# Score products of three attention layers: 64 contracted rows widened to 128

## The chip, the cores and the metric

One core of one Trainium2 chip runs the whole program. The metric is the device time in microseconds of one execution, the median of several runs.

## What is computed

The program is two small transformer blocks over one sequence of 512 tokens with 1024 features, all in float32. The first block has a dilated attention layer and a state-space (S5) layer; the second has a differential attention layer, an HGRN layer, a sliding-window layer and another differential layer, each followed by a feed-forward part. The change touches the scores of the attention layers alone, which the reference computes with 64 features a head:

```python
logits = jnp.einsum('bnqrhe,bnkrhe->bnrhqk', qs, kw, ...) * scale + bias      # dilated, 3 groups
s = jnp.einsum('bmqd,bmkd->bmqk', q[:, :, qs:ke], k[:, :, :ke])               # differential
s = jnp.einsum('bnqhgd,bnkhd->bnhgqk', q, kb)                                 # sliding window
```

After the scores come a bias, a softmax over the keys and the product with the values.

## The kernel before

Activations stand transposed in SBUF, features on the 128 partitions and 512 tokens in the free dimension. Matrix products of weights are made from two parts of each operand, a rounded high part and the remainder (the type F32R), in three products (`mm3`, L167 to L169). A projection (`projF_steps`) makes one block of 128 features by 512 tokens out of 8 times 3 such products and hands the PSUM tile to an epilogue on ScalarE or VectorE.

The 16 heads are taken in four quarters of four heads. A block of 128 features holds two heads, e = 0 on partitions 0 to 63 and e = 1 on 64 to 127. For every quarter there is a chain of projections (q, k, v) and an `attend` generator with eight steps, one for each of four query blocks and two pairs of heads; a step makes the scores of step i, transposes the probabilities of step i - 1 and multiplies those of step i - 2 with the values. `weave` interleaves the projections of what comes next (the fill) with the attend steps of what is there, in the order in which TensorE is to run them; a scheduler keeps to that order where dependencies and free tiles allow. Softmax goes through VectorE (bias and minimum, L474 or L805) and ScalarE (exponential, L477 or L807).

- **Dilated layer** (`dilated`, plain float32 scores). `project_q` (L554 to 557) writes one tile Q of 128 partitions by 2 blocks by 512 tokens, one ScalarE operation for each block. `products` multiplies rows 64e to 64e + 63 of Q and K: for group 0 one product of 128 or 256 keys for each head (L589), for the other two groups two products of 128 keys for each head (L593). There are 12 q projections (4 quarters, 3 groups), 24 blocks in all.
- **Differential layers** (`diff_attention`, two of them). `pack_q` (L868 to 876) writes for each head a tile half with the high part of q on the head's own 64 rows and the low part on the other 64. `pack_k` (L878 to 886) writes the high part of k on both halves (the copy is L886) and the low part on the head's own half alone; one tile `kl` holds the low parts of both blocks of a quarter. `packed_scores` then makes two products: 128 rows of q against the high part of k (L891), and the head's own 64 rows against the low part (L892), accumulated in PSUM.
- **Sliding layer** (`swa`). The same two products through `pair_scores`; its low part of k already stands on both halves. Its value products write 64 columns of the array at a time (L978); they do not change.

The tiles of q, k, v, bias, low parts, outputs and products (`self.g`) share one pool `gp` of 16 slots; a tile waits for a free slot, and a slot comes free with the last use of what it held. Projections share three PSUM buffers (`ps_mm`), scores two (`ps_sc`). Bias tiles come by DMAs on SP's queue (L461).

Of the kernel before, what the change touches and what calls it, by code (L numbers as in the profile page):

```python
# [11 lines left out]
F32 = mybir.dt.float32  # L12
F32R = mybir.dt.float32r
ACTF = mybir.ActivationFunctionType
ALU = mybir.AluOpType
AX = mybir.AxisListType

P = 128
S = 512
# [31 lines left out]
class Core:  # L51
# [454 lines left out]
    def dilated(self, w_in, d1, g_out, rest):  # L506


        nc = self.nc
        def col(which, g, q):  # L510
            c0 = which * 3072 + g * 1024 + q * 256
            return w_in[:, c0:c0 + 256]

        def view(ps, g):
            return ps if g == 0 else ps.rearrange("p (j r) -> p r j", r=4)

        def dst(t, m, g):
            return t[:, m, :] if g == 0 else t[:, m, :].rearrange("p (r j) -> p r j", r=4)
# [33 lines left out]
                yield  # L552

        def project_q(qd, g, t):  # L554
            t["q", g] = Q = self.g([P, 2, S], name="q")
            yield from self.projF_steps([col(0, g, qd)], 256,
                                        lambda m, ps: nc.scalar.mul(dst(Q, m, g), view(ps, g), -0.125))

        def project_k(qd, g, t):
            t["k", g] = K = self.g([P, 2, S], name="k")  # L560
# [12 lines left out]
        def attend(qd, g, t):  # L573
            st = t["st", g] = self.small([P, TB, 2, 4], f"st{g}", 2)
            O = t["O", g] = self.g([P, TB, 256], name="O")
            b = t["b0"] if g == 0 else self.g([P, 4, 256], name="b12")
            if g:
                self.bias_tile(b[:, :, 0:128], d1, 4 * qd, 4, 384 + 127, 128)
                self.bias_tile(b[:, :, 128:256], d1, 4 * qd, 4, 640 + 127, 128)

            def scores(i):
                u, m = divmod(i, 2)
                us, hs = slice(u * P, u * P + P), slice(2 * m, 2 * m + 2)

                def products(e, ps):
                    r = slice(64 * e, 64 * e + 64)
                    if g == 0:
                        k0 = max(0, u - 1) * P
                        nc.tensor.matmul(ps[:, :u * P + P - k0], lhsT=t["q", 0][r, m, us],  # L589
                                         rhs=t["k", 0][r, m, k0:u * P + P], start=True, stop=True)  # L590
                        return
                    for i in range(2):
                        nc.tensor.matmul(ps[:, i * P:i * P + P], lhsT=t["q", 1 + i][r, m, us],  # L593
                                         rhs=t["k", 1 + i][r, m, us], start=True, stop=True)

                return self.pair_scores(products, b[:, hs, :], lo(i), st[:, u, 0, hs], st[:, u, 1, hs], None)

            def lo(i):
                return P if g == 0 and i < 2 else 0

            def V(i, e, k):
                u, m = divmod(i, 2)
                c = slice((2 * m + e) * 64, (2 * m + e) * 64 + 64)
                return t["v", 0][:, u - 1 + k, c] if g == 0 else t["v", 1 + k][:, u, c]

            def values(i, pt):
                u, m = divmod(i, 2)
                po = self.psum([P, P], self.ps_av, "av")
                for e in range(2):
                    for k in range(lo(i) // P, 2):  # L610
                        nc.tensor.matmul(po[:, 64 * e:64 * e + 64], lhsT=pt[:, e, k, :], rhs=V(i, e, k),
                                         start=(k == lo(i) // P), stop=(k == 1))
                (nc.vector.tensor_copy if m else nc.scalar.copy)(O[:, u, m * P:m * P + P], po)

            for i, _ in enumerate(self.attend_pairs(8, scores, lo, values)):
                if (i + 1) * 8 // 10 > i * 8 // 10:
                    self.tick()
                yield
# [145 lines left out]
    def diff_attention(self, w_in, lam, subln, d2, lam_init, g_out, rest):  # L764

        nc = self.nc
# [15 lines left out]
        def project(qd, out):  # L782
            cs = lambda i, n: w_in[:, i * 1024 + qd * 256 + n.start:i * 1024 + qd * 256 + n.stop]
            V = self.g([P, TB, 256], name="v")
            yield from self.projT_steps(cs(2, slice(0, 256)),
                                        lambda tp, ps: nc.scalar.copy(V[:, 2 * tp:2 * tp + 2, :], ps))
            kl = self.g([P, 2, S], F32R, "kl")
            for m in range(2):
                bt = self.g([P, 2, S], name="bt")
                self.bias_tile(bt, d2, 4 * qd + 2 * m, 2, 127, S)  # L790
                q, kh = self.g([P, 2, S], F32R, "q"), self.g([P, 2, S], F32R, "kh")
                epi = lambda i, ps: (self.pack_k(ps, kh, kl[:, m, :]) if i else self.pack_q(ps, q))
                ms = slice(m * P, m * P + P)
                yield from self.projF_steps([cs(0, ms), cs(1, ms)], 256, epi)
                out.append((bt, q, kh, kl[:, m, :], V))

        def scores(bt, Q, Kh, Kl, V, u, m):
            nk = u * P + P
            nm, l = self.small([P, 2], "nm"), self.small([P, 2], "l")
            ss = []  # L800
            for e in range(2):
                ps = self.psum([P, S], self.ps_sc, "sc")
                s = self.t2([P, S], name="s")
                self.packed_scores(ps[:, :max(nk, 256)], Q, Kh[:, e, :], Kl, e, slice(u * P, nk), slice(0, max(nk, 256)))
                nc.vector.tensor_tensor_reduce(out=s[:, :nk], in0=ps[:, :nk], in1=bt[:, e, S - nk:], scale=1.0,  # L805
                                               scalar=3e38, op0=ALU.add, op1=ALU.min, accum_out=nm[:, e:e + 1])
                nc.scalar.activation(out=s[:, :nk], in_=s[:, :nk], func=ACTF.Exp, scale=-1.0,  # L807
                                     bias=nm[:, e:e + 1], accum_out=l[:, e:e + 1])
                ss.append(s)
            r1, f2 = self.small([P, 2], "r1"), self.small([P, 1], "f2")  # L810
            nc.vector.reciprocal(out=r1, in_=l)
            nc.vector.tensor_tensor(out=f2, in0=l[:, 0:1], in1=r1[:, 1:2], op=ALU.mult)
            nc.vector.tensor_tensor(out=f2, in0=f2, in1=nlam, op=ALU.mult)
            a = ss[0]
            nc.vector.scalar_tensor_tensor(out=a[:, :nk], in0=ss[1][:, :nk], scalar=f2, in1=a[:, :nk],
                                           op0=ALU.mult, op1=ALU.add)
            return a, r1
# [60 lines left out]
    def pack_k(self, ps, kh, kl):  # L878


        nc = self.nc
        for e in range(2):
            r, o = (slice(64 * i, 64 * i + 64) for i in (e, 1 - e))
            nc.scalar.copy(kh[r, e, :], ps[r, :])
            nc.vector.tensor_tensor(out=kl[r, :], in0=ps[r, :], in1=kh[r, e, :].bitcast(F32), op=ALU.subtract)  # L885
            nc.vector.tensor_copy(kh[o, e, :], kh[r, e, :])  # L886

    def packed_scores(self, ps, q, kh, kl, e, qs, ks):

        r = slice(64 * e, 64 * e + 64)  # L890
        self.nc.tensor.matmul(ps, lhsT=q[:, e, qs], rhs=kh[:, ks], start=True, stop=False)  # L891
        self.nc.tensor.matmul(ps, lhsT=q[r, e, qs], rhs=kl[r, ks], start=False, stop=True)  # L892

    def heads_by_quarters(self, project, attend, rest, n, period, tail, after):

# [15 lines left out]
    def swa(self, w_in, sinks, d2, g_out, rest):  # L911
        nc = self.nc
# [29 lines left out]
        def attend(qd, bq):  # L942
# [4 lines left out]
            def scores(i):  # L947
                u, m = divmod(i, 2)
                k0 = max(0, u - 1) * P
                hs = slice(2 * m, 2 * m + 2)  # L950
                sink = ns[:, 4 * qd + 2 * m:4 * qd + 2 * m + 2]
                nm, l, es = (self.small([P, 2], n) for n in ("nm", "l", "es"))

                def products(e, ps):
                    self.packed_scores(ps, Q[m], Kh[:, kv, :], Kl[:, kv, :], e, slice(u * P, u * P + P),
                                       slice(k0, k0 + 256))

                s = self.pair_scores(products, b0[:, hs, :], lo(i), nm, l, sink)
                nc.vector.tensor_tensor(out=es, in0=nm, in1=sink, op=ALU.subtract)
                nc.scalar.activation(out=es, in_=es, func=ACTF.Exp)  # L960
                nc.vector.tensor_tensor(out=es, in0=es, in1=l, op=ALU.add)
                nc.vector.reciprocal(out=es, in_=es)
                for e in range(2):
                    nc.vector.tensor_scalar(out=s[:, e, lo(i):], in0=s[:, e, lo(i):], scalar1=es[:, e:e + 1],
                                            scalar2=None, op0=ALU.mult)
                return s
# [647 lines left out]
```

## Time and profile before

| | us |
|---|---|
| median of 3 runs (lowest, highest) | 3721.05 (3717.48, 3723.71) |
| profiled execution | 3716.22 |
| its span, first to last instruction | 3714.3 |
| TensorE busy with products | 3647.3 (98%) |
| VectorE busy | 2206.8 (59%) |
| ScalarE busy | 1389.1 (37%) |
| GpSimd busy | 131.7 (4%) |

The profiler models the end of a product, so that products overlap in its records and a busy share near 100% does not say how fast they follow each other. The distance from one start to the next is what a product costs; the timeline gives these starts. A form such as "64\*128 64x256" is 64 contracted rows by 128 stationary columns, with 256 moving columns. Stages of the program by time: dilated layer about 20 to 720 us, first differential layer 1040 to 1300, sliding layer 2455 to 2620, second differential layer 3030 to 3290.

### The profile page before, as it was taken

The page shows a single profiled execution, that of the slowest core. Times are in us where ns is not written, and L with a number is a line of the kernel's source. Part 1 is how long each engine was busy: PE and PEld are TensorE (multiplying, and loading weights), DVE is VectorE, ACT ScalarE, POOL GpSimd, SP SyncE. Part 2 cuts the span into 40 slices and gives each one's busy share as a digit, 9 for nine tenths or more (in the row PEclk, how much of TensorE's full clock was granted, in tenths as well). Part 3 has the DMA queues.
Part 4 walks back from the last instruction along what each step waited for, and adds up shares of the span by engine and source line. Part 5 has one row for each costly group of instructions (what it writes and reads, how often), then busy time and mean ns, then how long its engine had stood idle before and what let it go on. Part 6 is the DMA issues. An engine that isn't in the chain of part 4 may idle for free. (4 is left out here: it accounts for less than half of the span.)

```text
span 3714.3 us, 49214 instructions
## 1 busy us (share of the span) xinstructions
PE 3647.3 (98%) x19511; PEld 3038.2 (82%) x19511; DVE 2206.8 (59%) x4701; ACT 1389.1 (37%) x2409; POOL 131.7 (4%) x191
## 2 busy tenths in 40 slices
PE   8999999889999999999999999999999999999999
PEld 7878787777777788889988888886888898788888
DVE  5677684555656744465778444657644556774445
ACT  4333333435344333234553222344322244432222
POOL 0000000010000100000000000000000000010000
PEclk9999999989999999999999999999999999999999
DMA  6234332465533222322212323321232243222322
GB/s 174 79 114 116 103 109 90 163 199 149 109 103 87 74 91 91 113 96 81 69 61 84 101 96 102 108 80 52 81 112 91 97 115 91 69 91 91 102 97 69
DMA packets 331806, 371.46 MB, mean 100 GB/s; under 512 B 37958, under 2 KB 268390, under 8 KB 331576
## 3 DMA queue, kind: packets, MB, share of 16 engines
q1 hardware_dynamic: 328064, 356.93, 31.6%
q0 software_dynamic: 3328, 11.14, 1.0%
q8 instruction: 153, 2.51, 0.3%
q14 instruction: 77, 0.63, 0.1%
q10 hardware_dynamic: 184, 0.26, 0.0%
HBM read 339.18 MB, written 29.10 MB: 99 GB/s over the span
## 5 line engine op out<-in xcount | busy, mean ns | idle before, releaser
L167 PE MATMUL mm<-xh,wh 128*128 128x512 f32 (+1 forms) x2488 | 943.8, 380 | 4.0 <-ACT wh L136 2.5
L168 PE MATMUL mm<-xl,wh 128*128 128x512 f32 (+1 forms) x2488 | 932.1, 375 | 3.0 <-DVE xl L137 3.0
L169 PE MATMUL mm<-xh,wl 128*128 128x512 f32 (+1 forms) x2488 | 931.2, 375 | 0.6 <-DVE wl L137 0.6
L137 DVE TENSOR_TENSOR wl<-wr,wh 128x2048 fp32r<-128x2048 f32 x270 | 633.7, 2348 | 467.9 <-ACT wh L136 457.2
L136 ACT CAST wh<-wr 128x2048 fp32r<-128x2048 f32 x270 | 536.9, 1989 | 812.9 <-PE mm L169 427.6
L167 PEld LDWEIGHTS mm<-xh,wh 128*128 128x128 f32 x2488 | 472.4, 190 | 86.4 <-issue 4.0
L169 PEld LDWEIGHTS mm<-xh,wl 128*128 128x128 f32 x2488 | 472.3, 190 | 83.6 <-DVE wl L137 1.6
L168 PEld LDWEIGHTS mm<-xl,wh 128*128 128x128 f32 x2488 | 472.9, 190 | 82.3 <-DVE xl L137 3.5
L168 PE MATMUL mm<-wl,uh 128*128 128x512 f32 x1024 | 399.2, 390 | 0.0
L167 PE MATMUL mm<-wh,uh 128*128 128x512 f32 x1024 | 398.8, 389 | 0.0
L169 PE MATMUL mm<-wh,ul 128*128 128x512 f32 x1024 | 398.4, 389 | 0.0
L167 PE MATMUL mm<-wh,xh 128*128 128x256 f32 (+1 forms) x1088 | 321.2, 295 | 0.0
L168 PE MATMUL mm<-wl,xh 128*128 128x256 f32 (+1 forms) x1088 | 317.5, 292 | 0.0
L169 PE MATMUL mm<-wh,xl 128*128 128x256 f32 (+1 forms) x1088 | 316.9, 291 | 0.0
L320 DVE TENSOR_TENSOR h<-h,mm 128x512 f32<-128x512 f32 x256 | 174.3, 682 | 233.0 <-PE mm L169 232.9
L167 PEld LDWEIGHTS mm<-wh,uh 128*128 128x128 f32 x1024 | 192.2, 188 | 39.9
L169 PEld LDWEIGHTS mm<-wh,ul 128*128 128x128 f32 x1024 | 192.3, 188 | 39.7
L168 PEld LDWEIGHTS mm<-wl,uh 128*128 128x128 f32 x1024 | 192.3, 188 | 39.4
L167 PEld LDWEIGHTS mm<-wh,xh 128*128 128x128 f32 x1088 | 209.7, 193 | 5.3 <-ACT xh L136 1.1
L168 PEld LDWEIGHTS mm<-wl,xh 128*128 128x128 f32 x1088 | 209.5, 193 | 4.0 <-issue 1.2
L169 PEld LDWEIGHTS mm<-wh,xl 128*128 128x128 f32 x1088 | 209.3, 192 | 3.1 <-issue 0.4
L136 ACT CAST uh<-t 128x512 fp32r<-128x512 f32 x128 | 79.4, 621 | 189.3 <-DVE t L350 189.3
(375 smaller groups left out, 4762.8 us busy)
## 6 DMA issues: line engine op xcount, KB each, us to landing
wr<-in_w_up_dram SPq DMA_DIRECT2D x64, 1024.0 KB, 5.5
wr<-in_w_down_dram SPq DMA_DIRECT2D x64, 1024.0 KB, 5.1
wr<-in_attn_w_in_dram SPq DMA_DIRECT2D x40, 1024.0 KB, 5.1
wr<-in_da_w_in_dram SPq DMA_DIRECT2D x32, 512.0 KB, 5.3
wr<-in_w_ple_gate_dram SPq DMA_DIRECT2D x16, 1024.0 KB, 5.2
wr<-in_hg_w_in_dram SPq DMA_DIRECT2D x16, 1024.0 KB, 5.4
wr<-in_ssm_w_in_dram SPq DMA_DIRECT2D x8, 1024.0 KB, 7.0
wr<-in_da_w_in_dram SPq DMA_DIRECT2D x8, 1024.0 KB, 5.2
```

Of the source, the lines that this page charges most:

```text
L136: self.nc.scalar.copy(hi, src)
L137: self.nc.vector.tensor_tensor(out=lo, in0=src, in1=hi.bitcast(F32), op=ALU.subtract)
L167: nc.tensor.matmul(ps, lhsT=a[0], rhs=b[0], start=start, stop=False)
L168: nc.tensor.matmul(ps, lhsT=a[0], rhs=b[1], start=False, stop=False)
L169: nc.tensor.matmul(ps, lhsT=a[1], rhs=b[0], start=False, stop=stop)
L320: self.nc.vector.tensor_tensor(out=h[:, sl], in0=h[:, sl], in1=ps, op=ALU.add)
```

## The change

In the dilated layer the q projection writes two tiles instead of one, one for each block. Each has a half for each head, in which the head's own 64 rows hold q and the other 64 rows are set to zero by GpSimd; ScalarE writes the two halves by two operations of 64 rows. The score products take all 128 rows of Q and of K. In the differential layers `pack_k` copies the low part of k to the other 64 rows too, so that `kl` takes one tile for each block (two a quarter). Both products of `packed_scores` then take 128 rows, in the differential and in the sliding layer; the product of the low parts of q and k comes into the sum with that.

```diff
         def project_q(qd, g, t):
-            t["q", g] = Q = self.g([P, 2, S], name="q")
-            yield from self.projF_steps([col(0, g, qd)], 256,
-                                        lambda m, ps: nc.scalar.mul(dst(Q, m, g), view(ps, g), -0.125))
+            t["q", g] = Q = [self.g([P, 2, S], name="q") for _ in range(2)]
+            for q in Q:
+                for e in range(2):
+                    nc.gpsimd.memset(q[64 - 64 * e:128 - 64 * e, e, :], 0.0)
+
+            def epi(m, ps):
+                for e in range(2):
+                    r = slice(64 * e, 64 * e + 64)
+                    nc.scalar.mul(dst(Q[m][r], e, g), view(ps[r], g), -0.125)
+
+            yield from self.projF_steps([col(0, g, qd)], 256, epi)
...
-                    r = slice(64 * e, 64 * e + 64)
...
-                        nc.tensor.matmul(ps[:, :u * P + P - k0], lhsT=t["q", 0][r, m, us],
-                                         rhs=t["k", 0][r, m, k0:u * P + P], start=True, stop=True)
+                        nc.tensor.matmul(ps[:, :u * P + P - k0], lhsT=t["q", 0][m][:, e, us],
+                                         rhs=t["k", 0][:, m, k0:u * P + P], start=True, stop=True)
...
-            kl = self.g([P, 2, S], F32R, "kl")
             for m in range(2):
...
-                q, kh = self.g([P, 2, S], F32R, "q"), self.g([P, 2, S], F32R, "kh")
+                q, kh, kl = (self.g([P, 2, S], F32R, n) for n in ("q", "kh", "kl"))
...
-            nc.vector.tensor_tensor(out=kl[r, :], in0=ps[r, :], in1=kh[r, e, :].bitcast(F32), op=ALU.subtract)
+            nc.vector.tensor_tensor(out=kl[r, e, :], in0=ps[r, :], in1=kh[r, e, :].bitcast(F32), op=ALU.subtract)
             nc.vector.tensor_copy(kh[o, e, :], kh[r, e, :])
+            nc.vector.tensor_copy(kl[o, e, :], kl[r, e, :])
-    def packed_scores(self, ps, q, kh, kl, e, qs, ks):
-        r = slice(64 * e, 64 * e + 64)
-        self.nc.tensor.matmul(ps, lhsT=q[:, e, qs], rhs=kh[:, ks], start=True, stop=False)
-        self.nc.tensor.matmul(ps, lhsT=q[r, e, qs], rhs=kl[r, ks], start=False, stop=True)
+    def packed_scores(self, ps, q, kh, kl, ks):
+        self.nc.tensor.matmul(ps, lhsT=q, rhs=kh[:, ks], start=True, stop=False)
+        self.nc.tensor.matmul(ps, lhsT=q, rhs=kl[:, ks], start=False, stop=True)
```

## Rows read from the trace of the kernel before

**Rows 1.** Stretches: window, length, busy us of each engine, granted clock, DMA share, GB/s.

```profile
20.00:720.00 700.00, 695.97 (x3764) 551.76 (x3764) 453.54 (x1642) 262.83 (x566) 6.61 (x22) 1.00 0.38 108
1040.00:1300.00 260.00, 256.75 (x1399) 206.58 (x1398) 184.73 (x497) 117.53 (x286) 25.70 (x37) 1.00 0.31 88
2455.00:2620.00 165.00, 164.99 (x853) 115.19 (x853) 116.86 (x378) 78.84 (x222) 3.07 (x2) 1.00 0.21 61
3030.00:3290.00 260.00, 257.86 (x1411) 208.08 (x1411) 176.02 (x494) 119.25 (x292) 22.10 (x34) 1.00 0.29 80
```

**Rows 2.** Timeline, TensorE, sliding layer: start us, duration us, engine, line, tiles, form.

```profile
2483.55 0.39 PE L167 MATMUL mm<-xh,wh 128*128 128x512 f32 x1
2483.78 0.39 PE L168 MATMUL mm<-xl,wh 128*128 128x512 f32 x1
2484.01 0.28 PE L891 MATMUL sc<-kh,q 128*128 128x256 f32 x1
2484.21 0.38 PE L892 MATMUL sc<-kl,q 64*128 64x256 f32 x1
2484.52 0.50 PE L169 MATMUL mm<-xh,wl 128*128 128x512 f32 x1
2484.86 0.40 PE L167 MATMUL mm<-xh,wh 128*128 128x512 f32 x1
```

**Rows 3.** Timeline, TensorE, first differential layer.

```profile
1057.31 0.28 PE L891 MATMUL sc<-kh,q 128*128 128x256 f32 x1
1057.52 0.38 PE L892 MATMUL sc<-kl,q 64*128 64x256 f32 x1
...
1058.45 0.39 PE L167 MATMUL mm<-wh,xh 128*128 128x256 f32 x1
1058.68 0.28 PE L168 MATMUL mm<-wl,xh 128*128 128x256 f32 x1
1058.80 0.28 PE L169 MATMUL mm<-wh,xl 128*128 128x256 f32 x1
```

**Rows 4.** Timeline, TensorE, dilated layer, a pair of products of group 0.

```profile
124.97 0.39 PE L169 MATMUL mm<-xh,wl 128*128 128x512 f32 x1
125.29 0.70 PE L589 MATMUL sc<-k,q 64*128 64x256 f32 x2
125.91 0.55 PE L245 MATMUL tr<-ident,s 128*128 128x128 f32 x3
```

**Rows 5.** Timeline, TensorE, dilated layer, four products of groups 1 and 2.

```profile
151.19 0.71 PE L593 MATMUL sc<-k,q 64*128 64x128 f32 x4
151.83 0.66 PE L245 MATMUL tr<-ident,s 128*128 128x128 f32 x4
152.32 0.27 PE L245 MATMUL cT<-ident,cn 128*128 128x128 f32 x1
```

**Rows 6.** Timeline, TensorE, plain float32 products of 512 columns.

```profile
961.78 1.03 PE L450 MATMUL ps<-oh,rb 33*16 33x512 f32 x2
962.74 0.50 PE L167 MATMUL mm<-wh,xh 128*128 128x512 f32 x1
```

**Rows 7.** Tile sc: products of 64 rows, durations ns min/median/max, first and last start, forms.

```profile
L593 PE MATMUL sc<-k,q x256: 272/272/373, 144.0 to 681.3; 64*128 64x128 f32 x128
...
L892 PE MATMUL sc<-kl,q x192: 378/382/500, 1057.5 to 3258.7; 64*128 64x256 f32 x128, 64*128 64x384 f32 x32, 64*128 64x512 f32 x32
...
L589 PE MATMUL sc<-k,q x128: 272/376/480, 54.9 to 628.0; 64*128 64x256 f32 x96, 64*128 64x128 f32 x32
```

**Rows 8.** Lines L874, L886 and L1029, each alone: durations ns min/median/max.

```profile
L874 ACT ACTIVATE q<-mm x48: 587/592/596, 1041.6 to 3223.6; 64x512 fp32r<-64x512 f32 x48
...
L886 DVE CAST kh<-kh x32: 420/421/424, 1048.0 to 3236.0; 64x512 fp32r<-64x512 f32 x32
...
L1029 POOL MEMSET seg<- x1: 546/546/546, 1682.1 to 1682.1; 128x512 f32 x1
```

**Rows 9.** Timeline, SP's queue, bias tiles of the last quarter of the dilated layer.

```profile
636.55 5.28 SPq L461 DMA_DIRECT2D b<-bvd x8
```

More of the change, by code (lines that the diff above doesn't have):

```diff
@@ L585, in products @@
                 def products(e, ps):
-                    r = slice(64 * e, 64 * e + 64)
                     if g == 0:
                         k0 = max(0, u - 1) * P
-                        nc.tensor.matmul(ps[:, :u * P + P - k0], lhsT=t["q", 0][r, m, us],
-                                         rhs=t["k", 0][r, m, k0:u * P + P], start=True, stop=True)
+                        nc.tensor.matmul(ps[:, :u * P + P - k0], lhsT=t["q", 0][m][:, e, us],
+                                         rhs=t["k", 0][:, m, k0:u * P + P], start=True, stop=True)
                         return
                     for i in range(2):
-                        nc.tensor.matmul(ps[:, i * P:i * P + P], lhsT=t["q", 1 + i][r, m, us],
-                                         rhs=t["k", 1 + i][r, m, us], start=True, stop=True)
+                        nc.tensor.matmul(ps[:, i * P:i * P + P], lhsT=t["q", 1 + i][m][:, e, us],
+                                         rhs=t["k", 1 + i][:, m, us], start=True, stop=True)
                 return self.pair_scores(products, b[:, hs, :], lo(i), st[:, u, 0, hs], st[:, u, 1, hs], None)
@@ L790, in project @@
                 self.bias_tile(bt, d2, 4 * qd + 2 * m, 2, 127, S)
-                q, kh = self.g([P, 2, S], F32R, "q"), self.g([P, 2, S], F32R, "kh")
-                epi = lambda i, ps: (self.pack_k(ps, kh, kl[:, m, :]) if i else self.pack_q(ps, q))
+                q, kh, kl = (self.g([P, 2, S], F32R, n) for n in ("q", "kh", "kl"))
+                epi = lambda i, ps: (self.pack_k(ps, kh, kl) if i else self.pack_q(ps, q))
                 ms = slice(m * P, m * P + P)
                 yield from self.projF_steps([cs(0, ms), cs(1, ms)], 256, epi)
-                out.append((bt, q, kh, kl[:, m, :], V))
+                out.append((bt, q, kh, kl, V))
         def scores(bt, Q, Kh, Kl, V, u, m):
@@ L803, in scores @@
                 s = self.t2([P, S], name="s")
-                self.packed_scores(ps[:, :max(nk, 256)], Q, Kh[:, e, :], Kl, e, slice(u * P, nk), slice(0, max(nk, 256)))
+                self.packed_scores(ps[:, :max(nk, 256)], Q[:, e, u * P:nk], Kh[:, e, :], Kl[:, e, :],
+                                   slice(0, max(nk, 256)))
                 nc.vector.tensor_tensor_reduce(out=s[:, :nk], in0=ps[:, :nk], in1=bt[:, e, S - nk:], scale=1.0,
@@ L954, in products @@
                 def products(e, ps):
-                    self.packed_scores(ps, Q[m], Kh[:, kv, :], Kl[:, kv, :], e, slice(u * P, u * P + P),
+                    self.packed_scores(ps, Q[m][:, e, u * P:u * P + P], Kh[:, kv, :], Kl[:, kv, :],
                                        slice(k0, k0 + 256))
```

## The prediction

> **What bounds the kernel.** I read the stretches first, because the change touches four stages and the share of the whole span says nothing about any of them [rows 1]. TensorE is recorded busy for 695.97 of 700 us in the dilated layer, 164.99 of 165 in the sliding one, 256.75 and 257.86 of 260 in the differential ones, at full granted clock (1.00, the level of 2.4 GHz). VectorE stands at 453.54 (65%), 116.86 (71%), 184.73 and 176.02 (71% and 68%), ScalarE below 50%. So TensorE sets the pace, and a product that starts the next one sooner shortens the stage, as long as the other two keep up. Since ends of products are modelled, the second view is the timeline of TensorE around a score, read from start to start.
>
> A stream of like products runs evenly: 0.23 us for 512 columns (2483.55, 2483.78, 2484.01) [rows 2], 0.12 us for 256 (1058.68, 1058.80) [rows 3]. Around a product of 64 rows it doesn't. The 64-row product of the sliding layer, 256 columns, holds the next one off for 0.31 us (2484.21 to 2484.52); the full-height product ahead of it takes 0.20 instead of 0.12, and the first one behind it 0.34 instead of 0.23 [rows 2]. Going from 128 rows to 64 and back is paid at both ends, on the engine that bounds, with nothing beside it. That is what the change takes away.
>
> **Part 1, low parts on both halves (differential and sliding layers).** From the start of L891 to the start of the second product behind the score there are 0.85 us (2484.01 to 2484.86); without changes of height they would be 0.12 + 0.12 + 0.23 = 0.47. So one 64-row product costs 0.38 us too much [rows 2]. In the differential layer the two heads follow each other: 1057.31 to 1058.68 is 1.37 us for five products that need 5 x 0.12 = 0.60, which is 0.77 for two, 0.385 each [rows 3]. There are 192 such products, 64 in each layer; I take the same price for the 64 of them with 384 and 512 columns, since what is lost is a change and not columns [rows 7]. That is 128 x 0.385 + 64 x 0.38 = 49.3 + 24.3 = 73.6 us. In the sliding layer some scores stand beside value products that fill only 64 columns of the array; those changes stay, and I take off 2 us.
>
> **Part 2, zero-padded queries (dilated layer).** Group 0 has 48 pairs of 256 columns and 16 of 128, the other groups 64 sets of four of 128 [rows 7]. The pair of 256 takes 0.62 us to the next start, and the product ahead of it 0.32 instead of 0.23 [rows 4]. What two full-height float32 products of 256 columns will take is in no row, so I bound it: 0.12 each if they ran as the F32R ones do [rows 3], 0.31 each if nothing but their height changed [rows 4]. The nearest row is a plain float32 pair of 512 columns, 0.96 us to the next start including one change at its end [rows 6]; less 0.09 that is 0.435 each, 0.22 for 256 columns, and this I take. The saving is 0.09 ahead, 0.62 - 0.44 = 0.18 within, and behind it up to the 0.11 of rows 2, of which I take 0.07 because transposes follow more often than projections: 0.34 x 48 = 16.3 us. At the bounds it is 9.6 us more or 8.6 us less. A set of four takes 0.64 us; transposes of the same 128 columns run at (152.32 - 151.83) / 4 = 0.12 [rows 5], so 0.16 within and again 0.09 + 0.07, 0.32 us. The 16 pairs of 128 pay the same changes: 80 x 0.32 = 25.6 us. Together 41.9 us.
>
> **What is added.** VectorE gets 32 copies of 64 x 512, 0.42 us each as the copy of the high part [rows 8], 6.7 us in each differential layer, whose span shrinks from 260 to about 235: VectorE goes to 191 of 235, 81%. In the sliding layer nothing is added, but 117 us now have to fit into some 143, 82%. Copies and sums of the scores stand in one queue there; each copy sends the reductions behind it off 0.42 us later, and TensorE waits for these one step on. I see no row for these waits; between nothing and 0.42 x 32 = 13 us in the differential layers I take 6 us for all three, nearer the lower end, because a step has 2 to 4 us of projections as cover.
> ScalarE makes 24 more operations of 64 x 512 at 0.59 us [rows 8], 14 us on top of 263 of 700: hidden behind the next block, since three PSUM buffers hold the projections; if that cover were gone, it would be those 14 us.
> GpSimd makes 48 memsets of 64 x 512. The one row of that width is 0.55 us [rows 8], so 26 us on an engine busy for 6.6 us of the stage. ScalarE's write into the tile doesn't wait for them, but the first score does; they are issued with the tile, a whole projection block (24 x 0.23 = 5.5 us) earlier. Queued behind them is only background work.
> Q takes two slots of 16 for one. By my count of live tiles in the code, the second to last quarters ask for 17 to 19 at a time while q is projected. What is late then is the ScalarE write of a projection, until the seventh or eighth score step has freed its queries; behind it one PSUM buffer of three. The pool is tight already: the last quarter's bias tiles are issued at 636.55 and take 5.28 us to issue [rows 9]. Bounds: nothing, or one block of 5.5 us in each of the last three quarters, 16.5 us. I take 4 us.
>
> **Sum.** 73.6 - 2 + 41.9 = 113.5 saved, 6 + 4 = 10 given back: 103.5 us. The profiled execution took 3716.2, of which 1.9 lie outside its span; it becomes 3612.7. The median of the runs shown is 4.8 us above it, so 3617 us is what I put down.
>
> **Rivals.**
> (a) *VectorE or ScalarE takes over in the differential and sliding layers.* For it: 81 to 82% of VectorE on average, with scores, copies and weight splits in one queue. Against it: no TensorE idle in the sliding layer now [rows 1]. If half of part 1 is lost in waits, the gain is 103.5 - 37 = 67 us: 3654 us.
> (b) *The padding gains nothing, because the two halves already share the array.* A padded set would then take as long as the 64-row one does now, and only part 1 counts: 73.6 - 2 - 10 = 62 us, 3659 us. Against it: the pair of heads, on rows 0 to 63 and 64 to 127, needs 0.62 us for what is 0.44 one after the other [rows 4]. The Trainium skill, TensorE: Matmul & The Clock Gate, Part 3 (Packing small matmuls), says that products on different row groups run at the same time, which speaks against padding; by it the two should start almost together, and this trace shows them apart, so the rule gets little weight here.
> (c) *The pool of 16 stalls the dilated layer, and it is slower.* If the second q tile comes free only after the attend steps, the projection can't cover them any more, and each of the 24 q blocks leaves TensorE idle for its 5.5 us: 132 us against 113.5, 3721 - 113.5 + 132 = 3740 us. It decides when 21 of 24 blocks lose their cover. Against it: the first quarter asks for no more than 15, and TensorE's order has other projections to put in.
> (d) *The products are not issued at full height* (the zero rows are dropped, or the copy isn't used): 3721 plus the 10 us of what is added, 3731 us. Nothing speaks for it but that I haven't seen the instructions.
>
> **How the numbers follow.** Forecast 0.78, (a) 0.11, (b) 0.04, (c) 0.04, (d) 0.03. The forecast's own unknowns give 3721 - 113.5 - 9.6 = 3598 at the low end; at the high end 8.6 (float32 rate) + 7 (copies at 13) + 12.5 (pool at 16.5) less gain gives 3645. That range holds the forecast and the better part of (a), so I leave it there. About 7.4 us, 0.2%, is what a measurement of this kernel can tell from no change; forecast, (a) and (b) are all faster by more: 0.93. Within it 0.03, slower 0.04.
>
> **What would show it.** In the profile after, no row "64\*128" should stand under the scores; L169 to L891 to the next projection should run at 0.12 and 0.23 without a gap; the pair of 256 columns in the dilated layer should take near 0.44 instead of 0.62. The dilated stage should be some 35 to 42 us shorter, each of the other three about 22. If the sliding or differential stage shrinks by less than 15 us and TensorE shows waits for VectorE, (a) is right; waits around the q projections in the last two quarters point to (c). I am wrong if the starts are even and the stages are no shorter.

## The result, and the profile after

The changed kernel takes 3624.2 us in the median of four runs (3620.37 to 3632.09), the kernel before 3721.82 us in four (3717.48 to 3723.71): a ratio of 0.9742, 95% interval 0.9722 to 0.9762, 97.6 us less. The profiled execution is the longest of the four: 3632.09 us, span 3630.1 us.

The stretches of the changed kernel, each from its first score product to the end of its last, with the columns of [rows 1]:

```profile
55.00:646.50 591.50, 587.44 (x3383) 494.72 (x3382) 416.60 (x1593) 249.59 (x553) 21.97 (x52) 1.00 0.37 108
1030.00:1199.70 169.70, 165.44 (x1007) 143.97 (x1006) 132.98 (x423) 93.11 (x251) 17.15 (x28) 1.00 0.29 82
2416.00:2537.50 121.50, 121.34 (x730) 91.59 (x729) 97.39 (x345) 69.36 (x207) 1.16 (x1) 1.00 0.25 75
3004.60:3175.00 170.40, 165.65 (x1007) 143.98 (x1006) 132.96 (x423) 93.02 (x251) 17.23 (x28) 1.00 0.29 81
```

The same stretches of the kernel before:

```profile
54.90:681.60 626.70, 625.53 (x3386) 493.25 (x3385) 417.70 (x1592) 236.51 (x531) 3.33 (x16) 1.00 0.35 102
1057.10:1245.20 188.10, 186.64 (x1006) 146.70 (x1004) 131.30 (x413) 94.22 (x251) 16.84 (x28) 1.00 0.26 74
2461.30:2603.80 142.50, 142.49 (x729) 96.94 (x728) 98.24 (x345) 69.30 (x207) 1.40 (x1) 1.00 0.21 63
3070.90:3259.00 188.10, 186.64 (x1006) 146.72 (x1004) 131.30 (x413) 94.02 (x251) 16.87 (x28) 1.00 0.27 73
```

TensorE runs as many products as before in each (within three), and VectorE is busy for as long within 2 us; the stretches are shorter. Taken from the first start of a score product to the last start (the measure of the tables below; the rows of tile sc give both times), the dilated layer went from 626.4 to 591.2 us, the differential layers from 187.6 and 187.7 to 169.1 and 169.8, the sliding layer from 141.9 to 120.9. That is 35.2 + 18.5 + 17.8 + 21.0 = 92.5 us. The span shrank by 84.2 us only: the S5 stage, which the change does not touch, took 6.9 us longer in this execution (last section), and the stretches between stages make up the other 1.4 us.

The timeline of TensorE in the changed kernel, first differential layer, answers to [rows 3]:

```profile
1030.25 0.28 PE L899 MATMUL sc<-kh,q 128*128 128x256 f32 x1
1030.36 0.28 PE L900 MATMUL sc<-kl,q 128*128 128x256 f32 x1
1030.48 0.28 PE L899 MATMUL sc<-kh,q 128*128 128x256 f32 x1
1030.60 0.28 PE L900 MATMUL sc<-kl,q 128*128 128x256 f32 x1
1030.72 0.28 PE L167 MATMUL mm<-wh,xh 128*128 128x256 f32 x1
1030.84 0.28 PE L168 MATMUL mm<-wl,xh 128*128 128x256 f32 x1
```

Every start is 0.12 us behind the one ahead: 0.59 us for five products where there were 1.37. Two more places of the same view, a score of the sliding layer and a set of four of the dilated layer, answer to [rows 2] and [rows 5]:

```profile
2441.75 0.28 PE L899 MATMUL sc<-kh,q 128*128 128x256 f32 x1
2441.86 0.28 PE L900 MATMUL sc<-kl,q 128*128 128x256 f32 x1
2441.98 0.39 PE L167 MATMUL mm<-xh,wh 128*128 128x512 f32 x1
2442.21 0.40 PE L168 MATMUL mm<-xl,wh 128*128 128x512 f32 x1
...
146.06 0.39 PE L169 MATMUL mm<-xh,wl 128*128 128x512 f32 x1
146.28 0.60 PE L601 MATMUL sc<-k,q 128*128 128x128 f32 x4
146.72 0.60 PE L245 MATMUL tr<-ident,s 128*128 128x128 f32 x4
```

0.46 us from the first score product to the second product behind the score, for 0.85 before; the four products of 128 columns take 0.44 us to the next start, for 0.64 before, and the product ahead of them 0.22 instead of 0.32 [rows 4]. What was saved does not grow with the columns. In the differential layers, from the first of a pair's four score products to the transposes behind them, the median went from 1.14 to 0.48 us at 256 columns, from 1.37 to 0.70 at 384 and from 1.60 to 0.93 at 512: 0.66 or 0.67 us each time.

The waits of TensorE in the first differential layer of the changed kernel (engine, line, what for: us in total, times, longest us) show what came instead:

```profile
PE tr L245 <- DVE s L823: 3.2, 7, 0.6
PE tr L245 <- DVE h L310: 1.4, 2, 1.2
PE tr L245 <- DVE f L820: 0.7, 2, 0.3
PE av L838 <- DVE ot L844: 0.5, 3, 0.2
...
```

Transposes now wait seven times for VectorE's last step of the softmax (L823). Before, the same view has one such wait (the line is L815 there):

```profile
PE tr L245 <- DVE s L815: 0.5, 1, 0.5
```

In the dilated layer there is a new row too:

```profile
PE sc L597 <- DVE st L474: 2.7, 3, 1.5
```

### The profile page after: what moved, and what is told of

The parts are those of the page before. It is cut to its first block, busy times and chain, and to the rows that moved or that the text cites. A ratio compares the mean times of both kernels' runs of the same rounds, so it can differ in the third digit from the quotient of the medians.

```text
span 3630.1 us, 49360 instructions
## 1 busy us (share of the span) xinstructions
PE 3555.7 (98%) x19511; PEld 3036.7 (84%) x19511; DVE 2211.3 (61%) x4733; ACT 1401.7 (39%) x2433; POOL 158.0 (4%) x239
```

## The experiments

Theory: each change between 64-row and 128-row products has a price on TensorE, the parts add up, and what is given back are waits for VectorE. Rivals: the padding gains nothing; the price belongs to the 64-row product and not to the change; the waits come from the added copies, from shorter cover, or from the pool of 16 tiles.

**The two parts alone.** The kernel with the low parts on both halves but `project_q` and `products` of the dilated layer as before:

```diff
-            t["q", g] = Q = [self.g([P, 2, S], name="q") for _ in range(2)]
...
+            t["q", g] = Q = self.g([P, 2, S], name="q")
...
+                        nc.tensor.matmul(ps[:, :u * P + P - k0], lhsT=t["q", 0][r, m, us],
+                                         rhs=t["k", 0][r, m, k0:u * P + P], start=True, stop=True)
...
```

> The low parts on both halves alone, the dilated layer as before. If each change of height has its own price and the parts add up, the three stages give 18.5 + 21.0 + 17.8 = 57 us, as between the two profiles: 3664 us, ratio 0.985. If padding gains nothing and the low parts bring all of it: 3624 us, ratio 0.974.

3658.59 us, ratio 0.9836 (0.9821 to 0.985): 62.0 us less than the 3720.6 us before. The differential stages take 169.1 and 169.9 us, the sliding one 120.9, as in the changed kernel, and the dilated one 626.5.

The other half, the zero-padded queries alone, is the kernel before with `project_q` and `products` of the change:

```diff
-            t["q", g] = Q = self.g([P, 2, S], name="q")
...
+            t["q", g] = Q = [self.g([P, 2, S], name="q") for _ in range(2)]
+            for q in Q:
+                for e in range(2):
+                    nc.gpsimd.memset(q[64 - 64 * e:128 - 64 * e, e, :], 0.0)
...
-                        nc.tensor.matmul(ps[:, :u * P + P - k0], lhsT=t["q", 0][r, m, us],
-                                         rhs=t["k", 0][r, m, k0:u * P + P], start=True, stop=True)
+                        nc.tensor.matmul(ps[:, :u * P + P - k0], lhsT=t["q", 0][m][:, e, us],
+                                         rhs=t["k", 0][:, m, k0:u * P + P], start=True, stop=True)
...
```

> The zero-padded queries alone, differential and sliding layers as before. If the parts add up, the dilated layer gives its 35 us: 3687 us, ratio 0.9905. If the two halves of the array already share the work and padding gains nothing: 3722 us or a little more, ratio 1.00.

3683.33 us, ratio 0.9901 (0.9887 to 0.9916): 37.3 us less. Only the dilated stage is shorter, 591.4 us. 62.0 and 37.3 make 99.3 against 97.6 for both: the parts add up, and rival (b), that the padding gains nothing, falls.

**Does the price belong to the change of height?** The kernel before, with the products of both heads grouped by height:

```diff
...
             for e in range(2):
...
-                self.packed_scores(ps[:, :max(nk, 256)], Q, Kh[:, e, :], Kl, e, slice(u * P, nk), slice(0, max(nk, 256)))
+                nc.tensor.matmul(pss[e][:, :n1], lhsT=Q[:, e, u * P:nk], rhs=Kh[:, e, :n1], start=True, stop=False)
+            for e in range(2):
+                r = slice(64 * e, 64 * e + 64)
+                nc.tensor.matmul(pss[e][:, :n1], lhsT=Q[r, e, u * P:nk], rhs=Kl[r, :n1], start=False, stop=True)
...
```

> The kernel before with the differential layers' products put in another order: both heads' 128-row products, then both heads' 64-row products, so two changes of height for two heads instead of four. If the price belongs to the change (0.38 us for going there and back), 64 round trips fall away: 24 us, 3696 us, 12 us in each differential stage (187.6 to about 176). If it belongs to the 64-row product itself, nothing: 3721 us.

3695.34 us, ratio 0.9937 (0.9921 to 0.9953); the differential stages 174.8 and 175.0, 12.8 and 12.7 us less than before, 0.40 us for each of the 64 pairs. Its timeline at the place of [rows 3]:

```profile
1060.38 0.40 PE L804 MATMUL sc<-kh,q 128*128 128x256 f32 x2
1060.71 0.38 PE L807 MATMUL sc<-kl,q 64*128 64x256 f32 x2
1061.02 0.38 PE L167 MATMUL mm<-wh,xh 128*128 128x256 f32 x1
1061.24 0.28 PE L168 MATMUL mm<-wl,xh 128*128 128x256 f32 x1
```

The same four score products, two of them still of 64 rows, take 0.86 us to 1061.24 instead of 1.37. But this run changed two things. One round trip of two went, and the two products of 64 rows now stand next to each other, on the two halves of the rows and into two PSUM tiles, and there they run side by side: their row, two products, lasts 0.38 us, as long as one of them alone, and the next start is 0.31 us behind, as it was behind one [rows 2]. Wherever the two stand together, 54 times of 64, they start 3 or 4 ns apart. So the 0.40 us a pair are not the price of a round trip alone, and that they come near its 0.38 is chance. At the place shown 0.51 us went; less the 0.12 us that a product of 256 columns takes in the stream, which the second one no longer needs, about 0.39 are left for the round trip. This is an estimate from these starts, and waits took a part of the gain back.

That the price belongs to the change and not to the product of 64 rows is shown by the kernel before. In its dilated layer a set of four such products takes 0.64 us to the next start [rows 5], and two sets that follow each other without a change between them take 1.09:

```profile
489.10 1.16 PE L593 MATMUL sc<-k,q 64*128 64x128 f32 x8
490.19 0.44 PE L245 MATMUL tr<-ident,s 128*128 128x128 f32 x2
```

Four more products of 64 rows cost 0.45 us, 0.11 each, which is the pace of full-height products of 128 columns (0.44 us for four in the changed kernel). The Trainium skill, TensorEngine Tiling (Array Packing), Tiling Modes, Key Properties, says that changing the tiling mode drains TensorE. A price at each change agrees with that, though no trace here shows the drain itself.

**The tighter pool.** The kernel before with the queries in two tiles and no padding:

```diff
-            t["q", g] = Q = self.g([P, 2, S], name="q")
+            t["q", g] = Q = [self.g([P, 2, S], name="q") for _ in range(2)]
...
-                                        lambda m, ps: nc.scalar.mul(dst(Q, m, g), view(ps, g), -0.125))
+                                        lambda m, ps: nc.scalar.mul(dst(Q[m], 0, g), view(ps, g), -0.125))
...
```

> The kernel before with the queries of a quarter in two tiles, one for each block (only the first half of each is used), without padding and without memsets; the products stay at 64 rows. If the 6 us by which the dilated layer fell short come from the tighter pool, this kernel is slower than before by 3 to 8 us: 3725 to 3730 us. If they come from shorter cover alone: 3722 us, unchanged.

3721.18 us against 3720.6, ratio 1.0004 (0.9994 to 1.0013); the dilated stage took 625.0 us, for 626.4. Two tiles for one cost nothing that can be measured here. In the changed kernel the waiting for slots can be seen, on the engine that has the time. The memset's line there:

```profile
L559 POOL MEMSET q<- x48: 517/520/632, 21.2 to 600.0; 64x512 f32 x48
...
its engine sat idle before it (us, times) until:
  PE sc L597: 85.0, 2
  PE sc L601: 35.8, 3
...
who waited for it (us, times):
  POOL w L1358: 1.8, 1
```

GpSimd stands for 121 us until score products have freed the tile, and only its own next background memset ever waits for it.

**The copies, or the cover?** The changed kernel with the new copy on ScalarE:

```diff
-            nc.vector.tensor_copy(kl[o, e, :], kl[r, e, :])
+            nc.scalar.copy(kl[o, e, :], kl[r, e, :])
```

> The changed kernel with the new copy of the low part on ScalarE instead of VectorE. If the copies in VectorE's queue make the new waits of the differential layers (about 5 us in each), it is faster than the changed kernel by 4 to 8 us: 3616 to 3620 us. If the waits come from the shorter cover alone: 3624 us, unchanged. If ScalarE gets late in turn: 3630 us.

3626.32 us, ratio 0.9747 (0.9733 to 0.9762): not told apart from the changed kernel. The stages tell more than the total: where nothing in them was changed, the differential and sliding stages repeat within 0.2 us from profile to profile, the dilated one within 1. Here the differential ones take 168.4 and 168.5 us, 0.7 and 1.3 less. In the first of them the waits have moved: value products wait five times for L844 (2.7 us), and a transpose only once for L823. Next, a kernel without the copy, which leaves the low part of k out of these scores; the second product reads the high part again:

```diff
-            nc.vector.tensor_copy(kl[o, e, :], kl[r, e, :])
...
-                self.packed_scores(ps[:, :max(nk, 256)], Q[:, e, u * P:nk], Kh[:, e, :], Kl[:, e, :],
+                self.packed_scores(ps[:, :max(nk, 256)], Q[:, e, u * P:nk], Kh[:, e, :], Kh[:, e, :],
```

> The changed kernel without the new copies: the second product of the differential layers reads the high part of k on both halves in place of the low part (so the low part is left out of those scores). If the copies in VectorE's queue make the new waits, the two differential stages are 4 to 5 us shorter each than in the changed kernel (169.1 and 169.8 from first to last score product): 164 to 165. If the shorter cover makes them: 168 to 169 each, as with the copies on ScalarE (168.4 and 168.5).

3624.78 us, ratio 0.9747 (0.9731 to 0.9762); stages 166.8 and 167.6, 2.3 and 2.2 less. This lies between the two answers: the copies make a part of the waits, not most. Both copies of k on ScalarE:

```diff
-            nc.vector.tensor_copy(kh[o, e, :], kh[r, e, :])
-            nc.vector.tensor_copy(kl[o, e, :], kl[r, e, :])
+            nc.scalar.copy(kh[o, e, :], ps[r, :])
+            nc.scalar.copy(kl[o, e, :], kl[r, e, :])
```

> The changed kernel with the copies of the high and of the low part of k both on ScalarE (the high one straight from PSUM). If VectorE's load in its queue makes the waits, the differential stages fall to 165 to 167 us each. If the cover alone counts, they stay at 168 to 169, total 3621 to 3626 us.

3625.72 us, ratio 0.975 (0.9732 to 0.9768); stages 168.0 and 168.4. Taking the older copy off VectorE too brings no more than a few tenths over the run with one. Then more cover: every step behind the scores one later.

```diff
-            for i in range(8 + 3):
+            for i in range(8 + 4):
...
-                j = i - 1
+                j = i - 2
                 if 0 <= j < 8:
                     late[j] += turn(late[j][0], j % 4, j // 4),
-                j = i - 2
+                j = i - 3
...
-        self.heads_by_quarters(project, attend, rest, 14, 11, 0, 1)
+        self.heads_by_quarters(project, attend, rest, 14, 11, 1, 1)
```

> The changed kernel with the differential layers' transposes, value products and output turns one step later, so that each softmax chain has one more step of projections as cover. If shorter cover makes the waits, they go: 164 to 166 us from first to last score product in both stages and 6 to 10 us less in all, 3615 us. If the copies make them by holding VectorE's queue, the stages stay at 168 to 170.

3630.21 us, ratio 0.9759 (0.9742 to 0.9777); stages 169.6 and 169.6: no gain where 164 to 166 were expected. But the waits of TensorE are others. First differential layer of this run:

```profile
PE av L838 <- DVE ot L844: 3.2, 9, 0.5
PE tr L245 <- DVE h L310: 1.2, 1, 1.2
...
```

No transpose waits for L823 any more; the value products wait nine times instead for L844, the last reader of the one PSUM buffer that they have. The later turn did give cover, and the next wait took the time. So, with the later turn kept, the value products of odd query blocks go to the transposes' PSUM buffers:

```diff
-            po = self.psum([P, P], self.ps_av, "av")
+            po = self.psum([P, P], self.ps_tr if u % 2 else self.ps_av, "av")
...
```

> The changed kernel with the later turn of the run before it, and with the value products of odd query blocks in the PSUM buffers of the transposes, so that two can stand at a time. If the later turn helped and the single PSUM buffer took its gain back, the differential stages now fall to 165 to 167 us each, total about 3618 us. If the waits are VectorE's load, wherever they show: 168 to 170 us each, as before.

3622.13 us, ratio 0.973 (0.9715 to 0.9744); both stages 166.2 us, 2.9 and 3.6 less than the changed kernel. The later turn's gain was there, and the buffer had held it back. The same second buffer and the copy on ScalarE, without the later turn:

```diff
-            po = self.psum([P, P], self.ps_av, "av")
+            po = self.psum([P, P], self.ps_tr if u % 2 else self.ps_av, "av")
...
-            nc.vector.tensor_copy(kl[o, e, :], kl[r, e, :])
+            nc.scalar.copy(kl[o, e, :], kl[r, e, :])
```

> The changed kernel with the copy of the low part on ScalarE and the value products of odd query blocks in the transposes' PSUM buffers. With both causes of the waits eased, 166 us in each differential stage and 3617 to 3620 us; if the transposes now wait for their buffers instead, 169 us or more.

3628.93 us, ratio 0.975 (0.9735 to 0.9764); stages 169.6 and 169.7. Without the later turn the second buffer is no help; the stages are 1.2 us longer than with the copy on ScalarE alone. The expectation had the transposes wait for their buffers then. They wait for L823, as in the changed kernel:

```profile
PE tr L245 <- DVE s L823: 3.9, 7, 0.8
```

Last, all of it, the later turn, the second buffer and both copies on ScalarE:

```diff
-            po = self.psum([P, P], self.ps_av, "av")
+            po = self.psum([P, P], self.ps_tr if u % 2 else self.ps_av, "av")
...
-            for i in range(8 + 3):
+            for i in range(8 + 4):
...
-                j = i - 1
+                j = i - 2
...
-                j = i - 2
+                j = i - 3
...
-            nc.vector.tensor_copy(kh[o, e, :], kh[r, e, :])
-            nc.vector.tensor_copy(kl[o, e, :], kl[r, e, :])
+            nc.scalar.copy(kh[o, e, :], ps[r, :])
+            nc.scalar.copy(kl[o, e, :], kl[r, e, :])
```

> The changed kernel with the later turn, two PSUM buffers for the value products and both copies of k on ScalarE. If load on VectorE and cover are two causes that add up, the differential stages fall below the 166.2 us of the run before, to 164 or 165 each, and the whole to about 3617 us, 0.2% under the changed kernel. If what is left is one chain that neither shortens: 166 us each, 3620 us.

3619.29 us, ratio 0.9728 (0.9715 to 0.9742); both stages 164.6 us, 4.5 and 5.2 us less than in the changed kernel. The two causes add up, nearly: both copies on ScalarE gave 1.1 and 1.4 us, the later turn with the second buffer 2.9 and 3.6. What is left of TensorE's waits in its first differential layer:

```profile
PE tr L245 <- DVE h L310: 1.3, 2, 1.1
PE av L838 <- DVE gl L137: 0.7, 1, 0.7
PE tr L245 <- DVE ot L844: 0.4, 2, 0.2
```

By its four stages it is the best version here, 9.5 us below the changed kernel; by the totals, whose intervals overlap, it is not told apart from it.

**The dilated layer's new waits.** The copy of the low part on ScalarE, and the dilated layer's keys out of PSUM on ScalarE as well:

```diff
-                                        lambda m, ps: nc.vector.tensor_copy(dst(K, m, g), view(ps, g)))
+                                        lambda m, ps: nc.scalar.copy(dst(K, m, g), view(ps, g)))
...
```

> The changed kernel with the copy of the low part on ScalarE and, in the dilated layer, the keys' way out of PSUM on ScalarE too (24 copies of 0.69 us less on VectorE). The dilated stage has new waits of scores for VectorE at the start of three quarters. If VectorE's queue is late there through its load, the stage falls from 591.2 to about 587 to 589 us from first to last score; if the waits come from the order in which background work is queued, it stays at 591. Total 3618 to 3624 us.

3625.82 us, ratio 0.9743 (0.9727 to 0.9759); the dilated stage 592.2 us. 24 copies of 0.69 us less for VectorE, 16.6 us, did not move the waits (2.7 us, three times, 1.5 the longest, as in the changed kernel), so its load is not what makes them. The timeline of the changed kernel at the start of a quarter shows the place:

```profile
391.21 0.59 PE L597 MATMUL sc<-k,q 128*128 128x256 f32 x2
...
391.64 0.38 PE L245 MATMUL tr<-ident,s 128*128 128x128 f32 x2
...
392.96 0.35 DVE L1379 TENSOR_SCALAR w<-w,nsgn 128x256 f32<-128x256 f32 x1
393.23 0.17 DVE L1184 TENSOR_TENSOR w<-w,w 128x16 f32<-128x16 f32 x1
393.32 0.42 DVE L474 CUSTOM_DVE_ANT_0 s<-sc,b 128x256 f32<-128x256 f32 x1
...
393.80 0.70 PE L597 MATMUL sc<-k,q 128*128 128x256 f32 x2 [0.86 <-DVE st L474]
```

The score products are done before 391.9, and their bias step L474 begins at 393.32, behind nine small operations from 392.12 on of the background work for the S5 tables (L1182 to L1187, L1379). That VectorE's fixed order makes the wait is read from this place; no run moved the background work, so it stays an argument.

## Why the prediction was right

**What bounds.** Right. TensorE set the pace, and starts closer together made the stages shorter at the same number of products.

**Part 1.** The price of 0.38 us a score was right: in the timeline above the gap is gone at the places that the prediction named. Taking one price for 256, 384 and 512 columns was right too: a pair of heads lost 0.66 or 0.67 us at each width before the transposes began, besides what the product behind paid, and the set of eight shows that the price is that of a change and not of the product. The prediction had 73.6 - 2 = 71.6 us before waits; 18.5 + 17.8 + 21.0 = 57.3 arrived in the profiled stages, 62.0 in the medians of part 1 alone.

**Part 2.** The float32 rate was the one taken: the pair of 256 columns takes 0.43 us (391.21 to 391.64) for the 0.44 of the sum, so the bounds on either side were not needed. Of 41.9 us, 35.2 arrived in the stage and 37.3 in the medians of part 2 alone. 2.7 us stand as new waits in the view. A pair of 256 columns between a projection and transposes gave just the 0.34 us of the sum (from the start of the product ahead to the second start behind, 1.11 and 0.77 us in the two traces, 24 times). But 13 pairs stand between value products of 64 columns, and these went from 0.99 to 0.79 only, which is 1.8 us less than the sum had for them. About 2 us are left that no row explains.

**What is given back** is the term of the sum that was mis-sized. The sum had 6 us of waits and 4 us for the pool. The pool cost nothing: the run with two tiles and no padding stays within its interval of 1.0, and where tiles are late, only GpSimd waits. The waits were more. The sliding layer gave 21.0 of its 24.3 - 2. The differential layers should have given 24.6 each and gave 18.5 and 17.8, so 6.1 and 6.8 us went back in each, where the sum had 6 for all three layers. The step that failed is "nearer the lower end, because a step has 2 to 4 us of projections as cover": the cover itself shrank by 0.77 us a pair of heads, the chain from scores to transposes had little to spare, and the single PSUM buffer of the value products stood right behind. The runs split it: without the copies 2.3 us come back in the first layer, with a later turn and a second buffer 2.9, with the later turn, the buffer and the copies on ScalarE 4.5. The other 1.6 stay open.

Of the rivals, (a) happened at a small scale, 12.9 us in the differential layers and nearly nothing in the sliding one, where the prediction had set its mark at a loss of half. (b) fell with the padding alone. The Trainium skill, TensorE: Matmul & The Clock Gate, Part 3 (Packing small matmuls), has products on different row groups at the same time. In the dilated layer the trace does not agree: four products, two on each half, took 0.64 us, and the same four over all rows 0.44. In the grouped run it does: two products on the two halves started 3 or 4 ns apart. So the prediction's ground against (b), that the two halves do not overlap, was right for the dilated layer alone. In the grouped run the two heads write two PSUM tiles, in the dilated layer one; no run changed this by itself, so the reason is not shown. (c) and (d) did not occur.

The forecast of 3617 us was 7.2 us under the median: 113.5 - 103.5 = 10 us given back in the sum, against 113.5 - 92.5 = 21 by the stages. That the median came as near as 7.2 is in part luck: it fell by 97.6 us, 5 more than the stages that the change touches, with an S5 stage that varies by itself.

## What to carry to other kernels

Read the distance from start to start around a product of another height, not its busy time: where products of 64 rows are mixed into a stream of 128-row ones, going there and back cost TensorE 0.38 us here, and zero rows or a second copy of the operand are cheaper than the change when other engines have room. Where a change of height has to stay, put the products of 64 rows next to each other: they then pay it once, and two on different halves ran side by side in the grouped run. When one experiment changes two things, as that one did, look at the single starts before its number is taken for either. When a change takes time out of the bounding engine, its gain is given back by the chains that this time used to cover; look for the wait that stands behind the one you remove (here the PSUM buffer behind the transposes), since a later turn without the second buffer, and the second buffer without the later turn, showed no gain.

## What the runs showed of the hardware

The S5 stage runs the same instructions in all of these kernels, and its length is not the same. From the first product of its states to the last, windows of the kernel before, of the changed kernel, and of the kernel with the keys' copies on ScalarE (columns as in [rows 1], the granted clock third from the end):

```profile
773.30:890.90 117.60, 102.37 (x539) 89.86 (x540) 65.15 (x76) 45.09 (x46) 10.65 (x21) 0.85 0.51 156
```

```profile
738.60:863.10 124.50, 111.08 (x540) 96.98 (x540) 65.06 (x77) 45.21 (x46) 10.65 (x21) 0.78 0.48 147
```

```profile
739.80:853.50 113.70, 101.07 (x539) 88.13 (x539) 64.01 (x76) 45.12 (x46) 10.65 (x21) 0.86 0.51 160
```

Between 0.78 and 0.86 of granted clock the stage takes 124.5 to 113.7 us: TensorE waits there again and again, falls to its lower level of 1.2 GHz and comes back to 2.4, and for how much of the stage differs from execution to execution. The kernel before with two query tiles, whose total is unchanged, had 124.8 us there. Whole executions show the same. Of the 36 executions of the kernel before that were timed beside the experiments, the nine with a mean granted clock of 0.991 or 0.992 took 3713.6 to 3715.5 us, the thirteen with 0.988 or 0.989 took 3720.6 to 3724.7. So the scatter of some 10 us in the totals goes with the clock; that the S5 stage makes most of it is read from the profiled executions alone. The attention stages run at 1.00 throughout and repeat within 0.2 us (the dilated one within 1), which made them the better measure for effects of 2 to 5 us.
